# Products dealt by each step's own work, evictions in two steps, and reordered products in the prologue and MLP of a stick-breaking attention layer

## The chip, the cores and the metric

One core of a Trainium2 chip runs the whole program. The metric is the device time of one execution in microseconds (us), the median of three runs. TensorE (PE) multiplies, VectorE (DVE), ScalarE (ACT) and GpSimd (POOL) work elementwise, SyncE (SP) issues the transfers (DMAs). Matrix products are written to eight banks of PSUM of 128 x 512 floats.

## What is computed

The layer works on 2048 tokens of 1024 numbers. A combined projection gives queries, keys and values of 12 heads of 64, and queries of four heads that attend to 256 memory tokens. Its output is projected, normalised, and goes through an MLP with a squared ReLU and a second normalisation.

```python
proj = x @ w_in_sb                                   # q, k, v, q_mem
z = q_blk @ k.T * scale                              # per head, causal
log_stay = where(strict, log_sigmoid(-z), 0)
later = reverse_cumsum(log_stay) - log_stay
w = where(strict, exp(log_sigmoid(z) + later), 0)    # stick-breaking weights
mix = w @ v
mem_out = softmax(q_mem @ k_mem.T * scale) @ v_mem
x = layer_norm(ALPHA * x + concat(mix, mem_out) @ w_out)
h = square(relu(x @ w_up))
out = layer_norm(ALPHA * x + h @ w_down)
```

## The kernel before

Every operand of a product is split into two half-precision parts, high and low, and a product takes three passes (`PASSES`, line 183): high by high, high by low, low by high. So a unit of projection, 128 output columns for a chunk of 512 tokens, is 3 x 8 = 24 matmuls of 128 x 512 (`proj_cols`, line 246). Its result in PSUM is split into two half-precision tiles by two instructions, ACT for the high part and DVE for the low part, which reads the high one (`split_ps`, line 159).

**Prologue.** Memory keys and values, the transposed x of the four chunks, and for each chunk the projections of heads pair 0 (`proj_v`, `proj_k`, `proj_q`) followed by two of the eight blocks of memory attention (`mem_attend`, line 336: query projection of a block, scores, exponentials, split, transposes by DMA, value products). The order of this part is the scheduler's; inside, each engine runs its own queue in order. Weights of pair 0 are loaded in the order v, k, q; those of the memory queries are loaded when `mem_attend` is first entered.

**Attention** (`attention`, line 492) is written out by hand in steps, and each engine keeps that order. A step is one pair of heads, 128 queries and up to 512 keys: two scores into two of four banks `z` (`score`), a sigmoid by ACT (`stay`), a running product by DVE (`scan`), and in the next step the split and transpose of the weights (`spread`; by DMA, or by PE in two of four steps of a diagonal block). Four steps make a block of 512 by 512; its value products (`gather`, 24 matmuls) come `BEHIND` = 4 steps after. Six pairs of heads have 40 steps each, 10 blocks, of which four are diagonal. In iteration n stand, in this order: what was put off to n (`later`), score and sigmoid of n + 1, scan of n, spread of n - 1, and then a share of the filling work.

The filling work is projections of the next pair and, in the last two pairs, of their own later chunks and of the output (`out_proj`). It is given as segments: a list of blocks, a share `done` of the steps by which it is to be finished, and units. A step gets products in proportion to a weight:

```python
starts[len(steps)] = units, [FILL[t.i] if t.diag else 1.0 for t, _ in mine], done
...
so_far = sum(weight[:n + 1 - begin]) if n < N else full
while spent < total * min(1.0, so_far / full):
```

A unit's eviction is put off by one step: `later(1, lambda: split_ps(hi, lo, pp, ISQ))`, ACT and DVE in the same step, in front of that step's sigmoid and scan. Values take three steps: ACT copies and DVE takes differences (`copy`, line 394), ACT and POOL split, SP transposes. Two banks `pj` hold products in attention.

**MLP** (lines 785 to 946). Up and down are done by seven products in place of eight on blocks of 2 x 2, with sums before and after. `up` (line 778) uses three banks for one pair of hidden column blocks; `down` (line 866) three banks for one row of 128 tokens; sums out of PSUM are DVE's. Eight groups of weights, two halves of the tokens; in the first half the weights are also split, on ACT and DVE, and stored; in the second they are read back. The last group of each half uses eight plain products.

## Time and profile before

| | |
|---|---|
| runs | 2463.18 us median of 3 (2460.62 to 2464.71) |
| the profiled execution | 2465.01 us, its span 2463.3 us, mean granted clock 0.967 |
| busy | PE 2265.9 us, DVE 1702.5, ACT 1182.8, POOL 1034.2 |
| prologue, with the first eight steps of pair 0 | 0 to 249.1 us |
| pairs 0 (from its ninth step) to 3 | 249.1 to 764.7 us |
| last two pairs | 764.7 to 1104.8 us |
| MLP, first and second half | some 1180 to 1850 us, 1850 us to the end |

In a window's row stand its stretch and length, the busy time of PE, PE's weight loads, DVE, ACT and POOL with counts, PE's granted clock, DMA's busy share and GB/s. In a timeline's row stand start and length, engine, line, operation, tiles, count, and in brackets the idle time before it and what ended that. Lines are those of the kernel before.

### The profile page before, as it was taken

What the parts mean: (1) busy time and instruction counts of PE and PEld (TensorE: products, weight loads), DVE (VectorE), ACT (ScalarE), POOL (GpSimd) and SP (SyncE); (2) the same over time, 40 slices, a digit from 0 to 9 for tenths busy, and PEclk for the clock granted to TensorE, in tenths of its full rate; (3) what the DMA queues carried; (4) which work ended last, traced back from release to release, by engine and by line L of the source; (5) the groups of instructions that cost most, each with busy time, mean ns of one, the idle gap of its engine ahead of it and who ended that gap; (6) DMA issues with size and microseconds to landing.
All of it is one profiled execution on the core that took longest, in us unless ns stands there. A gap on an engine that the chain in (4) does not pass through costs nothing.

```text
span 2463.3 us, 34394 instructions
## 1 busy us (share of the span) xinstructions
PE 2265.9 (92%) x12032; PEld 1006.3 (41%) x12032; DVE 1702.5 (69%) x2385; ACT 1182.8 (48%) x2577; POOL 1034.2 (42%) x826
## 2 busy tenths in 40 slices
PE   7987999999989899998699999989999999999996
PEld 5433333333434344334244444434444444444442
DVE  4545777777776776887988888787676444555448
ACT  4455767676675656553544543454334222233321
POOL 0000656555564544664664565355335222211123
PEclk9998999999999999999899999999999999999998
DMA  8234888878887787877743454244466333323311
GB/s 261 41 75 88 147 159 143 160 135 150 154 152 144 157 173 161 164 162 158 249 150 119 161 175 140 95 163 167 141 172 230 103 107 99 102 87 95 107 38 69
DMA packets 606284, 342.02 MB, mean 139 GB/s; under 512 B 487840, under 2 KB 544672, under 8 KB 606112
## 3 DMA queue, kind: packets, MB, share of 16 engines
q1 hardware_dynamic: 606112, 339.84, 55.1%
q8 instruction: 94, 1.54, 0.3%
q14 instruction: 78, 0.64, 0.1%
HBM read 143.65 MB, written 77.59 MB: 90 GB/s over the span
## 4 chain that ended last, share of the span: by engine, by line
PE 45%; DVE 13%; DMA 3%; issue 3%; ACT 2%; POOL 2%; SPq 0%; DVEq 0%; POOLq 0%; ACTq 0%
PE upb L799 8%; PE dnb L875 8%; PE dnc L875 6%; PE dna L875 5%; PE upc L799 4%; PE upa L799 4%; PE op L639 4%; DVE wr L683 2%; PE dn L875 2%; DVE rt L683 2%; DVE acc L603 1%; DVE e L455 1%; PE z L272 1%; PE av L332 1%; DMA wd<-in_w_down_dram 1%
## 5 line engine op out<-in xcount | busy, mean ns | idle before, releaser
L310 POOL TENSOR_TENSOR t<-e,t 128x512 f16<-128x512 f32 (+1 forms) x384 | 431.6, 1148 | 437.5 <-ACT t L309 369.6
L890 POOL TENSOR_TENSOR acc<-acc,v 128x512 f32<-128x512 f32 x168 | 223.2, 1339 | 527.9 <-DVE acc L888 388.4
L799 PEld LDWEIGHTS <-rt 128*128 128x128 f16 x2688 | 268.3, 100 | 390.6 <-issue 86.3
L875 PEld LDWEIGHTS <-hl 128*128 128x128 f16 x2736 | 267.7, 98 | 330.3 <-DVE hl L810 5.5
L455 DVE TENSOR_TENSOR_SCAN e<-z,carry,zero 128x512 f32<-128x512 f32 x288 | 347.8, 1261 | 9.5 <-ACT z L447 8.8
L447 ACT ACTIVATE z<-z 128x512 f32<-128x512 f32 (+1 forms) x480 | 226.3, 514 | 257.6 <-PE z L272 135.9
L799 PE MATMUL upb<-op,rt 128*128 128x512 f16 x1152 | 281.6, 395 | 37.3 <-DVE u L842 28.4
L875 PE MATMUL dnb<-wr,hl 128*128 128x512 f16 x1008 | 243.8, 379 | 0.0
L272 PE MATMUL z<-k,q 64*128 64x512 f16 (+3 forms) x1440 | 195.5, 353 | 50.2 <-DVE e L455 45.5
L309 ACT ACTIVATE t<-e 128x512 f16<-128x512 f32 (+1 forms) x384 | 226.4, 616 | 13.2 <-DMA w<-t 12.2
L799 PE MATMUL upa<-op,rt 128*128 128x512 f16 x768 | 185.4, 388 | 14.9 <-ACT u L832 10.7
L799 PE MATMUL upc<-op,rt 128*128 128x512 f16 x768 | 178.8, 380 | 0.9 <-DVE u L843 0.9
L639 PE MATMUL op<-wo,mx 128*128 128x512 f16 x720 | 172.2, 388 | 1.2 <-DVE acc L646 1.2
L875 PE MATMUL dnc<-wr,hl 128*128 128x512 f16 x672 | 167.9, 379 | 1.2 <-DVE acc L886 1.0
L875 PE MATMUL dna<-wr,hl 128*128 128x512 f16 x672 | 163.8, 380 | 3.3 <-DVE hl L810 3.2
L455 DVE TENSOR_TENSOR_SCAN e<-z,zero 128x128 f32<-128x128 f32 (+1 forms) x192 | 147.0, 805 | 22.7 <-ACT z L447 16.5
L332 PE MATMUL av<-w,v 128*64 128x512 f16 (+3 forms) x1440 | 148.9, 352 | 7.1 <-DMA w<-t 5.9
L252 PE MATMUL pq<-xT,wq 128*128 128x512 f16 x576 | 142.4, 389 | 8.2 <-DVE k L162 5.0
L252 PE MATMUL vp<-xT,wv 128*128 128x512 f16 x576 | 145.6, 395 | 2.3 <-ACT wv L143 2.3
L805 ACT ACTIVATE u<-u 128x512 f32<-128x512 f32 x96 | 60.4, 629 | 164.9 <-DVE u L843 73.1
L252 PE MATMUL kp<-xT,wk 128*128 128x512 f16 x576 | 138.9, 383 | 0.0
L908 ACT ACTIVATE v<-dna 128x512 f32<-128x512 f32 x56 | 32.4, 592 | 214.9 <-POOL acc L890 210.3
(176 smaller groups left out, 3211.1 us busy)
## 6 DMA issues: line engine op xcount, KB each, us to landing
keptdown<-wr SPq DMA_DIRECT2D x106, 256.0 KB, 3.3
wr<-keptdown SPq DMA_DIRECT2D x106, 256.0 KB, 2.9
keptup<-rt SPq DMA_DIRECT2D x48, 512.0 KB, 3.1
rt<-keptup SPq DMA_DIRECT2D x48, 512.0 KB, 3.4
wu<-in_w_up_dram SPq DMA_DIRECT2D x32, 512.0 KB, 4.5
wd<-in_w_down_dram SPq DMA_DIRECT2D x32, 512.0 KB, 4.0
x<-in_x_dram SPq DMA_DIRECT2D x16, 512.0 KB, 10.3
acc<-in_x_dram SPq DMA_DIRECT2D x16, 512.0 KB, 5.4
```

The costliest lines, as they stand in the source:

```text
L252: T.matmul(pp, lhsT=wt[:, a, k, :], rhs=xs(xT, c, b, k), start=n == 0, stop=n == 3 * KT - 1)
L272: T.matmul(banks[h], lhsT=q[rows, a, i * P:(i + 1) * P], rhs=keys(b)[rows], start=n == 0, stop=stop and n == 2)
L309: A.activation(hi, src, AF.Copy)
L310: G.tensor_tensor(lo, src, hi, ALU.subtract)
L332: T.matmul(av[h * HD:(h + 1) * HD, i0 * P:].rearrange("p (t n) -> p t n", n=P), lhsT=vv(h, a), rhs=pT(h, b)[:, i0:, :], start=first and n ...
L447: A.activation(t.z[:, :t.W], t.z[:, :t.W], AF.Sigmoid, scale=-SCORE)
L455: V.tensor_tensor_scan(t.e[:, t.W - 1::-1], t.z[:, t.W - 1::-1], zero[:, 0:1].broadcast_to([P, t.W]), init, ALU.mult, ALU.add)
L639: T.matmul(pp, lhsT=lhs, rhs=W[f"o{k}"][:, kb, n * C:(n + 1) * C], start=m == 0, stop=m == 3 * NKO - 1)
L683: V.scalar_tensor_tensor(lo, src, scale, hi, ALU.mult, ALU.subtract)
L799: T.matmul(bv, lhsT=r[:, a, k, :], rhs=operand(ops, s, b, k), start=start and n == 0, stop=n == 3 * HB - 1, skip_group_check=not start)
L875: mm = T.matmul(bank, lhsT=hl[s][:, g, a, i * P:(i + 1) * P], rhs=wr[r][:, g, b, :], start=start and m == 0, stop=m == 3 * n - 1, skip_gro ...
L890: G.tensor_tensor(sl, sl, u, ALU.add)
```

## The change

Six places change. Evictions of keys and queries go through `evict`: ACT in the step after the product, DVE a step later; the difference of values moves a step later too (`diff`). Products are dealt by `deal`: each step has a time of its own (`OWN`, plus `VALUES` in the step that holds gathers) and a share, and gets what is left of a common level. Among the segments, the second chunk's keys and queries of the last two pairs move into pair 3's segment, and the last two pairs get four joined segments in place of eight. In the prologue two blocks of memory attention come ahead of a chunk's own projections, and the bank `pt` is used for products too. In `up` the third sum is made as bc + u1 and then bb, and S4 comes ahead of A22. In `down` the products of two rows alternate.

```diff
+    def evict(hi, lo, pp):
+        def high():
+            A.activation(hi, pp, AF.Copy, scale=ISQ)
+            later(1, lambda: V.scalar_tensor_tensor(lo, pp, ISQ, hi, ALU.mult, ALU.subtract))
+        later(1, high)
...
-        later(1, lambda: split_ps(hi, lo, pp, ISQ))
+        evict(hi, lo, pp)
...
+            later(1, diff)
+
+        def diff():
             V.tensor_tensor(df[:, 1:], d[:, :C - 1], d[:, 1:], ALU.subtract)
             later(1, split)
...
-    FILL = (0.45, 0.45, 0.85, 1.1)
+    SHARE = (0.62, 0.89, 0.78, 0.96), 1.0
+    OWN = (3100, 4300, 2200, 2500), 1800
+    VALUES = 4200, 6500
...
+        share = [SHARE[0][t.i] if t.diag else SHARE[1] for t, _ in steps]
+        own = [OWN[0][t.i] if t.diag else OWN[1] for t, _ in steps]
+        for n, (t, _) in enumerate(steps):
+            if t.i == TB - 1 and n + 1 + BEHIND < N:
+                own[n + 1 + BEHIND] += VALUES[0] if t.diag else VALUES[1]
+
+        def deal(begin, count, total):
+            mine = range(begin, begin + count)
+            low, high = 0, 10 * (total + sum(own))
+            for _ in range(60):
+                rate = (low + high) / 2
+                parts = [max(0, rate * share[n] - own[n]) for n in mine]
+                low, high = (rate, high) if sum(parts) < total else (low, rate)
+            return [sum(parts[:k + 1]) for k in range(count)]
...
-                while spent < total * min(1.0, so_far / full):
+                while spent < min(total, plan[min(n - begin, len(plan) - 1)]):
...
         prod(bc, S1, rt1, True)
+        u3 = sbt("et", [P, C], F32, f"u3_{nm}")
+        V.tensor_tensor(u3, bc, u1, ALU.add)
...
         prod(bb, S3, rt3, False)
-        V.tensor_tensor(u3, bb, u1, ALU.add)
-        V.tensor_tensor(u3, bc, u3, ALU.add)
+        V.tensor_tensor(u3, bb, u3, ALU.add)
+        prod(bc, S4, r22, False)
+        V.tensor_tensor(u2, bc, u2, ALU.add)
         prod(bb, A22, rt4, False)
         V.tensor_tensor(u1, bb, u1, ALU.add)
-        prod(bc, S4, r22, False)
-        V.tensor_tensor(u2, bc, u2, ALU.add)
...
+    free_banks[0] = ("pj", "pj", "pt")
     for c in range(NC):
+        for _ in range(2):
+            next(members, None)
         for fn in (proj_v, proj_k, proj_q):
             run(fn(0, c))
-        for _ in range(2):
-            next(members, None)
+    free_banks[0] = ("pj",)
...
-            units += [unit(fn, q, 0) for q in (p + 1, p + 2) for fn in (proj_k, proj_q)]
+            units += [unit(fn, q, c) for c in range(2) for q in (p + 1, p + 2) for fn in (proj_k, proj_q)]
...
+    segments.append(([(a, 0), (b, 0)], 0.9, among(kq(a, 2), 0)))
+    segments.append(([(a, 1), (b, 1)], 0.95, among(kq(b, 2), 4) + kq(a, 3)[:1] + [flat[0][0]] + kq(a, 3)[1:] + take(2)))
+    segments.append(([(a, 2), (b, 2)], 0.95, kq(b, 3) + [once(gamma)] + take(8)))
+    final = take(14)
+    segments.append(([(a, 3), (b, 3)], 0.95, final))
```

In `down` the loop over two rows i now runs once for each kind of product, in the order A11, A12, S2, S1, S3, S4, A22, where it ran A11 and A12 of each row and then the five others of each row; S1 is added to the rows of x from its bank by DVE, and u3 by POOL as before.

Counted in the order of PE, a full block of pair 1 (third chunk, last block) has 8, 9, 8 and 9 products in its four steps before; now it has 12, 3, 12 and 11, the 3 right behind the gathers. Pair 3 has 288 products before and 384 now, the last two pairs' first eight steps 91 and 43.

The first place is DVE's queue in pair 1, where the query unit of pair 2's first chunk is evicted (`q2_0` from its bank `pq2_0`) among the scans of pair 1's third chunk (`e1_2_0_i_h`: step i, head h). Before:

```order
L455 SCALAR_TENSOR_TENSOR e1_2_0_0_0_4589<-z1_2_0_0_0_4522,carry_4461,zero_76 128x512
L455 SCALAR_TENSOR_TENSOR e1_2_0_0_1_4591<-z1_2_0_0_1_4523,carry_4461,zero_76 128x512
L162 SCALAR_TENSOR_TENSOR q2_0_4478<-pq2_0_4477,q2_0_4478 128x512
L455 SCALAR_TENSOR_TENSOR e1_2_0_1_0_4625<-z1_2_0_1_0_4579,carry_4461,zero_76 128x512
L455 SCALAR_TENSOR_TENSOR e1_2_0_1_1_4627<-z1_2_0_1_1_4580,carry_4461,zero_76 128x512
```

Now:

```order
L466 SCALAR_TENSOR_TENSOR e1_2_0_0_0_4585<-z1_2_0_0_0_4513,carry_4444,zero_76 128x512
L466 SCALAR_TENSOR_TENSOR e1_2_0_0_1_4587<-z1_2_0_0_1_4514,carry_4444,zero_76 128x512
L466 SCALAR_TENSOR_TENSOR e1_2_0_1_0_4612<-z1_2_0_1_0_4575,carry_4444,zero_76 128x512
L466 SCALAR_TENSOR_TENSOR e1_2_0_1_1_4614<-z1_2_0_1_1_4576,carry_4444,zero_76 128x512
L466 SCALAR_TENSOR_TENSOR e1_2_0_2_0_4651<-z1_2_0_2_0_4602,carry_4444,zero_76 128x512
L466 SCALAR_TENSOR_TENSOR e1_2_0_2_1_4653<-z1_2_0_2_1_4603,carry_4444,zero_76 128x512
L260 SCALAR_TENSOR_TENSOR q2_0_4503<-pq2_0_4502,q2_0_4503 128x512
L466 SCALAR_TENSOR_TENSOR e1_2_0_3_0_4687<-z1_2_0_3_0_4641,carry_4444,zero_76 128x512
```

The eviction stood between the scans of steps 0 and 1 and stands between those of steps 2 and 3, since the unit ends a step later and is evicted two steps after its end.

The second place is PE's queue at the end of the prologue: the scores of the last block of memory attention (`zm1_3_3`), and the first score of attention (`z0_0_0_0_0`). Before:

```order
L272 LDWEIGHTS qm1_2_1828
L272 MATMUL zm1_3_3_2004<-kvm_83,qm1_2_1828 128x256
L272 LDWEIGHTS q0_0_648
L272 MATMUL z0_0_0_0_0_2133<-k0_0_618,q0_0_648 128x128
L272 LDWEIGHTS q0_0_648
L272 MATMUL z0_0_0_0_1_2134<-k0_0_618,q0_0_648 128x128
```

Now (the lines left out are 8 key and 24 query products of pair 0's last chunk, each with its weight load):

```order
L280 LDWEIGHTS qm1_2_1739
L280 MATMUL zm1_3_3_1915<-kvm_83,qm1_2_1739 128x256
L252 LDWEIGHTS wk0_572
L252 MATMUL kp0_3_2064<-xT03_0_506,wk0_572 128x512
...
L252 LDWEIGHTS wq0_577
L252 MATMUL pq0_3_2091<-xT03_1_536,wq0_577 128x512
L280 LDWEIGHTS q0_0_944
L280 MATMUL z0_0_0_0_0_2133<-k0_0_914,q0_0_944 128x128
```

Nothing stood between the last memory scores and attention; now 32 products do.

The third place is DVE's queue in the MLP's first half, third group: splits of down weights (`wr`) and up weights (`rt`), and the additions of the third sum (`u3`) from the banks `upb` and `upc`. Before:

```order
L683 SCALAR_TENSOR_TENSOR wr0_4_4_14259<-t2_d0_5_14634,wr0_4_4_14259 128x512
L683 SCALAR_TENSOR_TENSOR wr0_4_6_14261<-t4_d0_4_14435,wr0_4_6_14261 128x512
L683 SCALAR_TENSOR_TENSOR wr0_4_5_14260<-t3_d0_5_14636,wr0_4_5_14260 128x512
L683 SCALAR_TENSOR_TENSOR wr0_4_6_14261<-t4_d0_5_14638,wr0_4_6_14261 128x512
L683 SCALAR_TENSOR_TENSOR rt0_6_14926<-wu0_6_0_14914,rt0_6_14926 128x512
L810 TENSOR_TENSOR hl0_4_0_14248<-r_0_4_14355,hl0_4_0_14248 128x512
L842 TENSOR_TENSOR u3_0_4_14372<-upb0_4_14301,u1_0_4_14315 128x512
L843 TENSOR_TENSOR u3_0_4_14372<-upc0_4_14302,u3_0_4_14372 128x512
```

Now:

```order
L714 SCALAR_TENSOR_TENSOR wr0_4_4_14259<-t2_d0_5_14634,wr0_4_4_14259 128x512
L714 SCALAR_TENSOR_TENSOR wr0_4_6_14261<-t4_d0_4_14435,wr0_4_6_14261 128x512
L869 TENSOR_TENSOR u3_0_4_14343<-upc0_4_14302,u1_0_4_14315 128x512
L714 SCALAR_TENSOR_TENSOR wr0_4_5_14260<-t3_d0_5_14636,wr0_4_5_14260 128x512
L714 SCALAR_TENSOR_TENSOR wr0_4_6_14261<-t4_d0_5_14638,wr0_4_6_14261 128x512
L714 SCALAR_TENSOR_TENSOR rt0_6_14926<-wu0_6_0_14914,rt0_6_14926 128x512
L841 TENSOR_TENSOR hl0_4_0_14248<-r_0_4_14357,hl0_4_0_14248 128x512
L874 TENSOR_TENSOR u3_0_4_14343<-upb0_4_14301,u3_0_4_14343 128x512
```

The addition from `upc` moved ahead of three splits; the one from `upb` stands behind the same splits as before.

## Rows read from the trace of the kernel before

**Rows 1.** The page, part 1: busy us, share of the span, instructions.

```profile
PE 2265.9 (92%) x12032; PEld 1006.3 (41%) x12032; DVE 1702.5 (69%) x2385; ACT 1182.8 (48%) x2577; POOL 1034.2 (42%) x826
```

**Rows 2.** Windows of the prologue; columns as told above.

```profile
90.00:191.00 101.00, 89.24 (x484) 39.73 (x481) 55.59 (x158) 54.66 (x164) 3.56 (x3) 0.92 0.41 78
191.00:249.10 58.10, 40.07 (x243) 17.75 (x243) 32.47 (x79) 32.25 (x98) 7.49 (x7) 0.79 0.40 82
```

**Rows 3.** Windows of pairs 0, 1, 2 and 3.

```profile
249.10:356.10 107.00, 100.32 (x652) 40.50 (x649) 82.95 (x88) 77.06 (x192) 66.85 (x60) 1.00 0.87 159
356.10:490.40 134.30, 124.29 (x824) 51.36 (x822) 100.76 (x117) 93.23 (x239) 79.77 (x73) 1.00 0.83 150
490.40:624.40 134.00, 125.56 (x834) 51.95 (x831) 99.49 (x116) 92.37 (x238) 79.76 (x73) 1.00 0.80 146
624.40:764.70 140.30, 127.87 (x811) 51.54 (x812) 104.92 (x117) 97.12 (x252) 84.83 (x77) 0.96 0.83 153
```

**Rows 4.** Windows of the last two pairs: steps 1-8, 9-24, 25-48, 49-80.

```profile
764.70:799.40 34.70, 32.97 (x219) 14.94 (x216) 20.80 (x33) 16.91 (x40) 11.16 (x11) 1.00 0.60 131
799.40:858.80 59.40, 50.09 (x339) 22.11 (x336) 45.11 (x53) 38.43 (x92) 30.88 (x28) 0.94 0.70 153
858.80:956.50 97.70, 97.53 (x604) 41.61 (x604) 67.63 (x81) 52.88 (x136) 45.57 (x42) 1.00 0.87 173
956.50:1104.80 148.30, 138.21 (x784) 56.45 (x784) 119.36 (x153) 82.81 (x192) 89.05 (x74) 0.97 0.75 155
```

**Rows 5.** Windows of the MLP's first and second half.

```profile
1300.00:1850.00 550.00, 518.48 (x2355) 234.62 (x2354) 442.68 (x587) 244.05 (x426) 252.64 (x173) 0.97 0.45 147
...
1920.00:2390.00 470.00, 470.00 (x2180) 213.05 (x2178) 229.03 (x355) 132.07 (x227) 99.95 (x80) 1.00 0.30 96
```

**Rows 6.** Waits of the whole span: us in total, times, longest us.

```profile
DVE q L162 <- ACT q L161: 71.1, 23, 7.7
...
PE z L272 <- DVE e L455: 45.5, 62, 3.1
...
PE pt L319 <- DVE w L162: 15.0, 15, 4.2
```

**Rows 7.** Timeline of pair 1, 423 to 430 us, ACT, DVE and PE.

```profile
423.39 1.07 ACT L447 ACTIVATE z<-z 128x512 f32<-128x512 f32 x2 [2.19 <-PE z L272]
...
425.58 0.60 ACT L161 ACTIVATE q<-pq 128x512 f16<-128x512 f32 x1
...
426.21 0.69 DVE L162 SCALAR_TENSOR_TENSOR q<-pq,q 128x512 f16<-128x512 f32 x1 [3.37 <-ACT q L161]
...
429.32 0.82 PE L272 MATMUL z<-k,q 64*128 64x512 f16 x5 [0.79 <-DVE e L455]
```

**Rows 8.** Timeline of pair 1, 405 to 411 us, PE.

```profile
405.38 2.78 PE L332 MATMUL av<-w,v 128*64 128x512 f16 x24
408.09 0.82 PE L272 MATMUL z<-k,q 64*128 64x512 f16 x6
408.84 2.12 PE L252 MATMUL kp<-xT,wk 128*128 128x512 f16 x9
410.89 0.82 PE L272 MATMUL z<-k,q 64*128 64x512 f16 x6
```

**Rows 9.** Timelines of the prologue, PE and ACT.

```profile
38.98 5.31 PE L252 MATMUL vp<-xT,wv 128*128 128x512 f16 x16 [2.29 <-ACT wv L143]
...
45.40 1.06 ACT L143 ACTIVATE wqm<-sqm 128x1024 f16<-128x1024 f32 x1 [2.77 <-DMA sqm<-in_w_in_sb_dram]
...
82.28 0.72 PE L272 MATMUL zm<-kvm,qm 64*128 64x256 f16 x7
...
108.98 1.48 PE L332 MATMUL avm<-pm,kvm 128*64 128x512 f16 x11
...
234.15 1.48 PE L332 MATMUL avm<-pm,kvm 128*64 128x512 f16 x11
```

**Rows 10.** Timeline of the MLP's first half, third group, PE.

```profile
1380.53 4.44 PE L799 MATMUL upb<-op,rt 128*128 128x512 f16 x12 [4.53 <-DVE u L842]
```

More of the change, by code (lines that the diff above doesn't have):

```diff
@@ L500, in attention @@
                     for i in range(TB)]
-            starts[len(steps)] = units, [FILL[t.i] if t.diag else 1.0 for t, _ in mine], done
+            starts[len(steps)] = units, len(mine), done
             steps += mine
         N = len(steps)
+        share = [SHARE[0][t.i] if t.diag else SHARE[1] for t, _ in steps]
[11 more added lines that the diff above has]
+            return [sum(parts[:k + 1]) for k in range(count)]
         work, spent, total = None, 0, 0
@@ L509, in attention @@
                     run(work)
-                units, weight, done = starts[n]
-                begin, spent, total, full = n, 0, sum(k for k, _ in units), sum(weight) * done
+                units, count, done = starts[n]
+                begin, spent, total = n, 0, sum(k for k, _ in units)
+                plan = deal(n, count, total / done)
                 work = (cost for _, u in units for cost in u())
@@ L526, in attention @@
             if work is not None:
-                so_far = sum(weight[:n + 1 - begin]) if n < N else full
-                while spent < total * min(1.0, so_far / full):
+                while spent < min(total, plan[min(n - begin, len(plan) - 1)]):
                     cost = next(work, None)
@@ new lines, in down @@
+            for i in two:
+                bc[i] = pst("bk", f"dnc{half}_{i}")
+                prod(i, bc[i], S1, T1, True)
+                add(i, c1, 1, bc[i], None)
+            for i in two:
+                prod(i, bb[i], S3, T3, False)
+                u3[i] = sbt("et", [P, C], F32, f"v3_{half}_{i}")
+                V.tensor_tensor(u3[i], bb[i], u1[i], ALU.add)
+                sl = acc[c1 * TB + i][:, C:]
+                G.tensor_tensor(sl, sl, u3[i], ALU.add)
+            for i in two:
+                prod(i, bc[i], S4, B22, False)
+                add(i, c0, 1, bc[i], u2[i])
@@ L927, in down @@
+            for i in two:
+                prod(i, bb[i], A22, T4, False)
+                add(i, c1, 0, bb[i], u1[i])
             yield
```

51 lines of the change are left out of this document (16 added, 35 removed).

## The prediction

> **What bounds the kernel now.** I read the page first, then the windows stage by stage, then the waits and timelines inside the stages. On the whole TensorE (PE) is busy 92% of the span and VectorE (DVE) 69% [rows 1], so time can come from PE's idle 197 us, from clock lost behind idle, and from nothing else unless the work itself shrinks, which it does not here. The windows say where that lies. In the prologue, from 90 to 249.1 us, PE is idle 11.8 and 18.0 us, at granted clocks of 0.92 and 0.79, means of the two levels 2.4 and 1.2 GHz [rows 2]. In pairs 0 to 3 (249.1 to 764.7 us) it is idle 6.7, 10.0, 8.4 and 12.4 us [rows 3]. In the last two pairs it is idle 1.7, 9.3, 0.2 and 10.1 us [rows 4]. In the MLP's first half 31.5 of 550 us are idle, in its second half none [rows 5]. The reader is to see that attention is nearly bound by PE, but that its idle comes in a regular way, and that 858.8 to 956.5 us shows the same loop with no idle at all.
>
> What makes the idle in attention is told by the waits: PE's scores wait 45.5 us for DVE's scans (a score bank comes free when its scan ends), and DVE waits 71.1 us in q's evictions alone for ScalarE (ACT) [rows 6]. One such place in full [rows 7]: the sigmoid of a score ends at 424.46 us (423.39 + 1.07), but DVE's queue holds an eviction in front of the scan, whose ACT half starts only at 425.58; so DVE idles 3.37 us, the scan starts at 426.8 instead of 424.5, and the score at 429.32 us finds its bank late.
>
> **The change, part by part.** I make the sum against the profiled execution, 2465.0 us (its span is 2463.3), which is 1.8 us above the median of the runs, 2463.2.
>
> *Evictions in two steps, and difference of values a step later* (`evict`, `diff`). Nothing is added: the same ACT and DVE instructions, DVE's half one step later. Queued behind the waiting DVE half was the scan, and behind that the score's bank. After the change the ACT half has a whole step (3.35 us, 134.3 over 40 [rows 3]) to get done. The price is that the product's bank is held one step longer; that is the fourth rival.
>
> *Products dealt by own work* (`deal`). The counts in the order of PE are my evidence: in full blocks of pair 1 the products per step were 8 to 10 in all four steps, also in the step whose gathers take PE another 2.71 us; now that step gets none to 3 and the others 7 to 12. PE's work per block stays: four scores at 0.75, gathers at 2.71, and products at 2.05 / 9 = 0.228 us each [rows 8]; for the block's some 34 products that is 3.0 + 2.7 + 7.8 = 13.5 us, while DVE has 100.8 / 134.3 of that time to fill [rows 3]. So the two parts together can take PE's idle, not more. In pairs 0 to 2 that idle is 25.1 us. Diagonal blocks keep some: PE's transposes wait for DVE there 15.0 us in 15 waits over the program [rows 6], and these are not touched. I leave 10 us: **-15**. Bounds: 0 (the waits only change place) and -25.
>
> *Second chunks moved into pair 3's segment, the last two pairs' segments joined.* Four units of 24 products move, 96. Pair 3: 127.9 us of PE, less 5.1 for its clock of 0.96 coming back, plus 96 x 0.228 = 21.9, plus 4.6 of idle left, is 149.3 against 140.3: **+9**. Last two pairs: PE's 33.0 + 50.1 + 97.5 + 138.2 = 318.8 us [rows 4], less 101 products (five more are left to the tail) at 0.228 = 23.0, less 3 of the some 7 us that the clocks of 0.94 and 0.97 cost, plus 11 of idle left of 21.3, is 303.8 against 340.1: **-36**. The five products in the tail: **+1**. Bounds for the three together: idle all left, clock as now, -1; idle all gone and clock full, -46. I take a value nearer the second, because the stretch at 858.8 shows the loop with 0.2 us of idle under a like load. The weight loads that move with the units go through SP and ACT at four per eight steps; DMA is busy 0.60 in the stretch that gets them and 0.87 where PE has no idle [rows 4], so I cost them at nothing; without that cover one cast on ACT is 1.06 us [rows 9], 8.5 us for eight.
>
> *Memory attention ahead of each chunk's own products, and a third bank for products.* Two effects. The first product now reads the memory queries' weights, which are loaded last: their cast runs at 45.40 to 46.46 us, while the first product runs at 38.98 now [rows 9]. The 24 products of that time come later, 24 x 0.2156 (470 us over 2180 in the MLP's second half [rows 5]) = +5.2. The other effect is the chain of the eight memory blocks (exponentials, split, transposes by DMA, values): their value products run from 108.98 to 234.15 us, seven intervals of 17.9 us [rows 9], and the kernel can't leave the prologue before the last. In the changed order the first block's scores stand behind 96 products from 46.5 us, so at 46.5 + 20.7 + some 5 of transposes = 72 us. Now they begin at 82.28 us [rows 9], and the chain starts some 10 us earlier (the 5.2 is in that). Between neighbouring blocks stand 61 to 63 products, 13.4 us, and a block's values, 1.48, with its scores taken as long: 16.4 us where 17.9 is now, seven times, is another 10. Against that the first attention steps still share ACT with the last two blocks. I take **-18** for the prologue. Bounds: +5 (the late weights alone) and -45 (idle of 29.8 us, and 89.2 x 0.08 + 40.1 x 0.21 = 15.5 us of clock [rows 2]).
>
> *MLP, up.* The third sum is now made as two additions at other places; the same count. In the first half PE stalls once per group of weights, 4.53 us in the row [rows 10], for an addition that stands behind four and more splits in DVE's queue (the third place in the order). In the changed order that addition stands behind the same splits, and an earlier one, for the product now in front, behind some of them; PE has 25 products between the two ends as before. So the stall is split in two and not removed: **0**, between +5 (one more DVE instruction, as long as the 0.69 of [rows 7], in front, seven times) and -10 (the shorter stalls on the second addition). *MLP, down.* The products of two rows alternate; PE hardly waits in these now, and in the second half not at all: **0**, hidden by a PE that is busy 470 of 470 us; if it were not, one exposed addition of 0.69 us per pair of rows, 28 times, would be +19.
>
> Sum: -15 + 9 - 36 + 1 - 18 = **-59**: 2406 for an execution like the profiled one, **2404** for the median.
>
> **The rivals.** (1) *Busy is not the floor.* Products in a row are 0.2156 us apart in the MLP [rows 5] and 0.228 in attention [rows 8], because every change of kind leaves a small hole that counts as busy. If steps with no products save that for the 2,000 or so products in attention, another 25 us go: 2379. The Trainium skill says in Perfetto Trace Analysis, Identifying the Most-Contended Engine, that busy time of matmuls is no good measure of the distance to the roof because they are pipelined; by that rule this case is the likelier, but our row at 858.8 with 97.5 us for 604 matmuls shows the holes staying where PE never idles. Chance 0.12.
>
> (2) *The chain of memory blocks stays as it is.* Each block's ACT work waits in ACT's queue for the block before; if the interval stays at 17.9 and the late weights eat the earlier start, the prologue gives 0: 2422. For it: the interval is as long at 191 to 235 us, where PE has little to do. Against: there, attention's first steps share ACT. Chance 0.13.
>
> (3) *The waits change place in attention.* With no products after the gathers, PE holds no score for 12 x 0.228 + 2.71 + 0.75 = 6.2 us; then DVE must catch up, and an eviction of 0.69 us before the scan is felt. Half of attention's 41 us would be left: 2424. Chance 0.10.
>
> (4) *Slower.* A product's bank is now held a step longer, and there are two. A unit of 24 products takes 2 steps at 12 per step, and its eviction two more, so a bank turns round in four steps, just as often as it is asked for; at 15 per step, as in pair 3, it is asked for sooner. If each of the 40 key and query units in attention then stalls PE by 2.5 us, +100: 2504. It decides from 1.5 us per unit on, where the 59 are gone. Against: the mean is 7 to 10 products a step. The Trainium skill (the same page, Optimization Strategy) warns that bubbles repeated in a regular way can mean too few PSUM buffers, which is this rival's mechanism; the trace has such bubbles on score banks [rows 6] and none named on product banks in attention. Chance 0.05. (5) *Nothing to measure*: gains and new stalls cancel, 2463. Chance 0.05.
>
> **How the numbers follow.** The forecast has 0.55, with a range of its own of 2386 to 2420 (the bounds of the prologue and of the last pairs, half used each). A measurement tells 0.2%, 4.9 us, from no change. Faster: 0.55 + 0.12 + 0.13 + 0.10 = 0.90; same 0.05; slower 0.05. From 2376 to 2440 takes in the forecast, and rivals 1 to 3 each by itself, not 2 and 3 together (2443), and leaves out some 0.15.
>
> **What would show it.** In the changed profile: DVE's waits for ACT in q and k, 71.1 us for q now, under 30; scores waiting for scans under 25 us; idle of PE in pairs 1 and 2 under 5 us each, pairs 1 and 2 near 128 us; pair 3 longer, near 149; from its end to the last scan near 304. The first product at 46 us, not 39; the last memory block's values near 213 us, not 234. In the MLP's first half a stall per group as now. I am wrong if PE waits for evictions at the first product of units (rival 4), if the memory blocks still end after 228 us, or if the MLP moves by over 10 us.

## The result, and the profile after

The changed kernel takes 2437.4 us (median of six executions, 2425.1 to 2442.7); the kernel before took 2463.9 beside it. The ratio is 0.989, with a 95% interval of 0.987 to 0.991: faster by 27 us where 59 were forecast. The sign held and the time lies inside the range. The size does not hold: attention, which carried most of the sum, gave less than half of its part, and other terms missed in both directions.

The profiled execution took 2425.1 us, its span 2423.4. It is the fastest of the six, so it shows 40 us of gain where the median shows 27; the experiments explain most of that. First the page's part 1, beside [rows 1]:

```profile
PE 2235.5 (92%) x12032; PEld 999.4 (41%) x12032; DVE 1700.9 (70%) x2385; ACT 1186.9 (49%) x2577; POOL 1022.0 (42%) x826
```

Then the windows, with the columns of [rows 2]: two of the prologue, pairs 0 to 3, four of the last two pairs, the MLP's first half, and everything behind the last scan.

```profile
90.00:180.00 90.00, 82.17 (x471) 36.86 (x470) 51.22 (x150) 52.78 (x163) 3.46 (x3) 0.96 0.43 82
180.00:237.60 57.60, 47.13 (x296) 21.19 (x296) 38.37 (x88) 36.50 (x106) 6.72 (x7) 0.97 0.47 94
237.60:344.90 107.30, 102.31 (x674) 42.48 (x676) 85.18 (x90) 77.01 (x197) 68.83 (x63) 0.98 0.88 159
344.90:477.10 132.20, 123.88 (x832) 52.35 (x829) 101.36 (x117) 92.42 (x239) 79.53 (x72) 1.00 0.86 152
477.10:606.00 128.90, 121.25 (x819) 51.53 (x819) 100.19 (x116) 91.38 (x238) 79.52 (x73) 1.00 0.83 152
606.00:760.00 154.00, 143.31 (x906) 60.30 (x903) 109.24 (x122) 98.90 (x255) 87.07 (x77) 0.98 0.76 138
760.00:791.20 31.20, 26.42 (x189) 12.29 (x190) 18.49 (x30) 16.32 (x39) 12.03 (x12) 0.95 0.64 135
791.20:846.10 54.90, 52.10 (x349) 22.57 (x344) 47.93 (x57) 38.81 (x93) 28.27 (x26) 1.00 0.90 203
846.10:937.30 91.20, 89.53 (x577) 37.90 (x576) 67.57 (x89) 54.79 (x139) 47.76 (x44) 1.00 0.90 182
937.30:1076.70 139.40, 127.56 (x731) 50.95 (x728) 114.69 (x140) 78.38 (x187) 87.50 (x73) 0.95 0.76 149
1275.00:1825.00 550.00, 518.48 (x2400) 236.24 (x2399) 447.27 (x618) 253.28 (x434) 252.66 (x179) 0.99 0.45 150
1076.70:2423.40 1346.70, 1253.86 (x5790) 569.68 (x5790) 926.85 (x1341) 515.25 (x869) 519.80 (x375) 0.98 0.42 136
```

Against [rows 3, 4] the reader sees four things. The ninth step of pair 0, the first behind the prologue's windows, comes at 237.6 us and not at 249.1. Pairs 0 to 2 gain 0, 2 and 5 us. Pair 3 grows by 13.7 us and the last two pairs shrink by 23.4 (340.1 to 316.7). In pair 3 and the last two pairs PE is still idle 10.7 and 21.1 us: products moved, idle did not go. And in the MLP's first half the same 518.48 us of PE hold 2400 products where 2355 were [rows 5], at a granted clock of 0.99 and not 0.97.

The waits of PE in the whole span (us in total, times, longest), beside [rows 6]:

```profile
PE pt L327 <- DVE w L162: 39.5, 23, 7.7
PE upc L830 <- DVE u L869: 15.4, 6, 2.7
PE z L280 <- DVE e L466: 13.4, 19, 1.7
```

and DVE's for the first halves of the two evictions:

```profile
DVE k L260 <- ACT k L259: 5.4, 5, 1.5
DVE q L260 <- ACT q L259: 4.8, 7, 1.2
```

DVE's wait for ACT in q's eviction fell from 71.1 to 4.8 us and the scores' wait for scans from 45.5 to 13.4, both as forecast. But PE's transposes of the diagonal weights (`pt`) now wait 39.5 us where they waited 15.0. The longest of these stands in the timeline of pair 3, SP, ACT, DVE and PE:

```profile
650.91 0.39 PE L327 MATMUL pt<-idf,e 128*128 128x128 f32 x2
...
652.49 0.57 SPq L138 DMA_DIRECT2D sk<-in_w_in_sb_dram  x1
...
656.91 1.06 ACT L143 ACTIVATE wk<-sk 128x1024 f16<-128x1024 f32 x1 [4.00 <-DMA sk<-in_w_in_sb_dram]
...
660.17 0.26 ACT L161 ACTIVATE w<-pt 128x128 f16<-128x128 f32 x1
...
660.46 0.29 DVE L162 SCALAR_TENSOR_TENSOR w<-pt,w 128x128 f16<-128x128 f32 x1 [8.54 <-ACT w L161]
...
661.53 0.87 PE L327 MATMUL pt<-idf,e 128*128 128x128 f32 x3 [7.74 <-DVE w L162]
```

The transposes at 650.91 fill the one bank `pt`. It comes free when ACT and DVE have split it, but in ACT's queue two casts of the key and query weights of one of the last pairs stand in front, and the first waits 4.00 us for its DMA. So the split runs at 660.17 and the next transposes at 661.53. Two more, of 3.5 us behind casts of the output's weights and of 5.2 us behind the layer norm's work, come about in this manner; the other 19 in attention are of 0.2 to 2.2 us.

### The profile page after: what moved, and what is told of

Its sections match the earlier page's. It is cut to its first block, busy times and chain, and to the rows that moved or that the text cites. A ratio compares the mean times of both kernels' runs of the same rounds, so it can differ in the third digit from the quotient of the medians.

```text
span 2423.4 us, 34527 instructions
## 1 busy us (share of the span) xinstructions
PE 2235.5 (92%) x12032; PEld 999.4 (41%) x12032; DVE 1700.9 (70%) x2385; ACT 1186.9 (49%) x2577; POOL 1022.0 (42%) x826
## 4 chain that ended last, share of the span: by engine, by line
PE 45%; DVE 13%; issue 4%; ACT 4%; DMA 3%; POOL 2%; SPq 1%; DVEq 0%; ACTq 0%; POOLq 0%
PE upb L830 7%; PE dnb L906 7%; PE dnc L906 5%; PE dna L906 5%; PE op L670 5%; PE upc L830 5%; PE upa L830 4%; DVE wr L714 2%; PE z L280 2%; PE av L340 2%; DVE rt L714 2%; DMA wd<-in_w_down_dram 1%; PE pq L252 1%; DVE acc L634 1%; PE kp L252 1%
## 5 line engine op out<-in xcount | busy, mean ns | idle before, releaser
L921 POOL TENSOR_TENSOR acc<-acc,v 128x512 f32<-128x512 f32 x112 | 149.9, 1342 | 488.9 <-DVE acc L919 432.4
L830 PE MATMUL upb<-op,rt 128*128 128x512 f16 x1152 | 268.1, 381 | 14.8 <-DVE u L874 8.3
L906 PE MATMUL dnb<-wr,hl 128*128 128x512 f16 x1008 | 235.9, 379 | 0.0
L280 PE MATMUL z<-k,q 64*128 64x512 f16 (+3 forms) x1440 | 184.3, 349 | 14.4 <-DVE e L466 13.4
L906 PE MATMUL dnc<-wr,hl 128*128 128x512 f16 x672 | 161.1, 379 | 1.0 <-DVE acc L917 0.7
L906 PE MATMUL dna<-wr,hl 128*128 128x512 f16 x672 | 154.4, 379 | 0.0
L252 PE MATMUL vp<-xT,wv 128*128 128x512 f16 x576 | 138.2, 384 | 0.0
L418 POOL TENSOR_TENSOR vt<-ve,vt 128x512 f16<-128x512 f32 x24 | 28.4, 1185 | 209.2 <-ACT vt L417 202.7
## 6 DMA issues: line engine op xcount, KB each, us to landing
x<-in_x_dram SPq DMA_DIRECT2D x16, 512.0 KB, 10.4
```

The lines of the kernel that those rows point to most:

```text
L252: T.matmul(pp, lhsT=wt[:, a, k, :], rhs=xs(xT, c, b, k), start=n == 0, stop=n == 3 * KT - 1)
L280: T.matmul(banks[h], lhsT=q[rows, a, i * P:(i + 1) * P], rhs=keys(b)[rows], start=n == 0, stop=stop and n == 2)
L830: T.matmul(bv, lhsT=r[:, a, k, :], rhs=operand(ops, s, b, k), start=start and n == 0, stop=n == 3 * HB - 1, skip_group_check=not start)
L906: mm = T.matmul(bank, lhsT=hl[s][:, g, a, i * P:(i + 1) * P], rhs=wr[r][:, g, b, :], start=start and m == 0, stop=m == 3 * n - 1, skip_gro ...
L921: G.tensor_tensor(sl, sl, u, ALU.add)
```

## The experiments

Each was timed beside the kernel before, which measured 2461.0 to 2463.1 us (2459.3 by one execution in the last set). "Behind the last scan" is the time from the last scan of attention to the end, in the profile.

**Is the first profile typical?** No edit, a second profile.

> The changed kernel again, nothing altered: the reference for the other runs on this chip. Theory A (the profiled execution of the changed kernel, 2425.1, was a lucky one and the typical one is its median, 2437.4): about 2437, and a second profile whose stages differ from the first by up to 12 us, spread over many places. Theory B (the first profile is typical and the median was pulled up by the chip): 2425 or so.

Measured: 2434.4 (2418.2 to 2442.6; ratio 0.9859 to 0.9906), and again the profiled execution was the fastest. Its attention agrees within 2 us with the first profile's, so no spread over many places, and neither theory as it was put: what differs between executions lies elsewhere. Two more executions, at the end, show where the larger part of it lies (below).

**Transposes behind the products.**

```diff
+            held = 0 <= n - 1 < N and steps[n - 1][0].diag and steps[n - 1][0].i not in DMA_DIAG
             if 0 <= n - 1 < N:
-                spread(steps[n - 1])
+                if not held:
+                    spread(steps[n - 1])
...
                 if n >= N:
                     run(work)
+            if held:
+                spread(steps[n - 1])
```

> The changed kernel, with one edit: in the first two steps of a diagonal block TensorE's transposes of the stick-breaking weights are issued after the step's products instead of before them. Theory A (the gain in attention was given back at these transposes, which waited 39.5 us for the split that frees their bank, where they waited 15.0 before the change): that wait falls under 20 us and the kernel gains 10 to 20 us on the changed kernel. Theory B (VectorE and ScalarE are late there anyhow, and a transpose that waits only shows it first): the wait goes to the next scores or to the gathers, and the time stays within 4 us. Theory C (the transposes' result is needed soon, four steps later): the gathers wait and it gets slower by 5 or more.

Measured: 2422.8 (ratio 0.9814 to 0.9858), 12 us below the changed kernel. In attention the transposes' wait fell from 35.0 to 13.0 us, the scores' rose from 10.4 to 19.4, and attention from the ninth step on took 829.3 us in place of 839.1. Theory A. In pairs 0 to 2 alone the transposes' wait fell from 11.3 us, in ten waits, to 1.0 us in two.

**The split first in its step.**

```diff
-        later(1, split)
+        due.setdefault(clock[0] + 1, []).insert(0, split)
```

> The changed kernel, with one edit: the split of the transposed weights, which frees their bank, is put first among the work that falls due in its step, so that casts of weights and the layer norm stand behind it in ScalarE's and VectorE's queues. Theory A (three or four long waits of 3.5 to 7.7 us come from a cast that stands in front of the split and waits for a weight's DMA): the longest wait of the transposes falls under 3 us, their sum by about 15 us, the time by 10 to 15. Theory B (the blocked queue itself is what costs; sigmoids stand behind the same cast): the wait moves to the scores, the time stays within 4 us.

Measured: 2427.3 (0.9848 to 0.9873); the transposes' longest wait is 1.1 us, their sum 13.5, but the scores wait 24.2, so attention gains only 5.5 us (833.6). Between A and B: of the 21.5 us that the transposes wait less, the scores wait 13.8 more. In pairs 0 to 2 the transposes' ten waits stay, at 9.1 us, so the work due ahead of the split in its step is not what makes these; with the transposes behind the products they go, as the run before shows.

**The MLP as before the change**: `up` and `down` put back whole, of which this is the third sum.

```diff
-        V.tensor_tensor(u3, bc, u1, ALU.add)
...
-        V.tensor_tensor(u3, bb, u3, ALU.add)
+        V.tensor_tensor(u3, bb, u1, ALU.add)
+        V.tensor_tensor(u3, bc, u3, ALU.add)
```

> The changed kernel with the MLP's two functions (sums in the up product, order of rows in the down product) as they were before the change. My forecast said that these are worth 0 (+5 to -10). The two profiles show the stretch behind the last scan 11.8 us shorter after the change. Theory A (that is the reordered additions): undoing them costs 8 to 14 us. Theory B (it is the run, its clock, or the shorter tail of attention): undoing them changes nothing beyond 4 us.

Measured: 2438.1 (0.9890 to 0.9916), 3.7 us above the changed kernel: by that number theory B. But its executions lie within 2.2 us of each other, where the changed kernel's lie 24 apart, and it needs 1358.2 us behind the last scan, as the kernel before (1358.5).

**Prologue, evictions, dealing, segments, undone one by one.**

```diff
-    free_banks[0] = ("pj", "pj", "pt")
     for c in range(NC):
-        for _ in range(2):
-            next(members, None)
         for fn in (proj_v, proj_k, proj_q):
             run(fn(0, c))
+        for _ in range(2):
+            next(members, None)
-    free_banks[0] = ("pj",)
```

> The changed kernel, with the prologue as before: each chunk's own products ahead of the memory blocks, and one kind of bank for products. Theory A (the prologue's part is a gain of its own, 11.5 us by the two profiles, where I forecast 18): 8 to 14 us slower than the changed kernel, first attention step at 249 us and not at 237. Theory B (it is given back later, since the first attention steps share ScalarE with the last memory blocks): within 4 us.

```diff
     def evict(hi, lo, pp):
-        def high():
...
-        later(1, high)
+        later(1, lambda: split_ps(hi, lo, pp, ISQ))
```

(keys and queries both go through `evict`; and the difference of values in the step of its copy)

> The changed kernel, with the evictions of keys and queries and the difference of values in one step again. Theory A (the eviction's two halves in one step are what made VectorE wait for ScalarE and so the scores for the scans): scores wait over 35 us for scans again (13 in the changed kernel) and it is 8 to 20 us slower than the changed kernel. Theory B (the dealing alone took those waits away): scores stay under 25 us and the time within 4 us. Theory C (with the dealing, the one-step eviction relieves the transposes): up to 8 us faster.

```diff
+    FILL = (0.45, 0.45, 0.85, 1.1)
...
-                while spent < min(total, plan[min(n - begin, len(plan) - 1)]):
+                so_far = sum(weight[:n + 1 - begin]) if n < N else full
+                while spent < total * min(1.0, so_far / full):
```

> The changed kernel, with the products dealt out by the old weights of a step (0.45, 0.45, 0.85, 1.1 in a diagonal block, 1.0 elsewhere); evictions and segments as changed. Theory A (the dealing gives the steps that gather no products and so removes waits for the scans): scores wait over 25 us, pairs 1 and 2 take 133 us or more each, 6 to 15 us slower than the changed kernel. Theory B (the dealing mostly moves the wait from the scores to the diagonal transposes): the transposes wait 15 to 20 us in place of 39.5, the scores 30 or more, time within 5 us.

```diff
-            units += [unit(fn, q, c) for c in range(2) for q in (p + 1, p + 2) for fn in (proj_k, proj_q)]
+            units += [unit(fn, q, 0) for q in (p + 1, p + 2) for fn in (proj_k, proj_q)]
...
-    segments.append(([(a, 0), (b, 0)], 0.9, among(kq(a, 2), 0)))
...
+    segments.append(([(a, 0)], 0.7, among(kq(a, 1), 0)))
+    segments.append(([(b, 0)], 0.7, among(kq(b, 1), 2)))
...
```

> The changed kernel, with the old segments: one chunk of one of the last two pairs in each, and the second chunks not moved to pair 3. Theory A (joining and moving is worth what the last 120 steps show, 13.6 us more in pair 3 and 23 less in the last two pairs): 6 to 14 us slower than the changed kernel, pair 3 near 140 us. Theory B (with evictions and dealing in place the last pairs have little idle to give): within 4 us.

Measured: prologue 2434.6, evictions 2456.8, dealing 2427.6, segments 2423.0, against 2434.4. Only the evictions are plain: 22 us slower without them, attention 861.1 us, scores waiting 34.9 us, theory A but for the size. With the old dealing the transposes wait 23.0 us and the scores 13.1, with the old segments 18.9 and 24.7. Undoing either seemed to make the kernel faster, by 7 and 11 us, which fits neither of their theories, and undoing the prologue to change nothing (theory B by the number), but executions of all four scattered; those without the two-step evictions fell into two groups, 2442 to 2446 and 2456 to 2460.

**What scatters them.** Three of the profiles so far showed one subtraction of 13.8 us on VectorE. The changed kernel itself shows it in the two last executions. Of the second, DVE, POOL and PE between the MLP's halves, and line 841's row of durations (min, median, max in ns):

```profile
1836.68 1.29 POOL L634 TENSOR_TENSOR acc<-acc,gb 128x512 f32<-128x512 f32 x1
...
1836.90 13.81 DVE L841 TENSOR_TENSOR hl<-r,hl 128x512 f16<-128x512 f32 x1 [8.70 <-ACT r L839]
...
1837.90 2.51 POOL L628 TENSOR_TENSOR acc<-acc,gb 128x512 f32<-128x512 f32 x2
...
1840.35 9.81 POOL L634 TENSOR_TENSOR acc<-acc,gb 128x512 f32<-128x512 f32 x8
...
1850.77 1.03 PE L906 MATMUL dna<-wr,hl 128*128 128x512 f16 x2 [9.23 <-DVE hl L841]
```

```profile
L841 DVE TENSOR_TENSOR hl<-r,hl x32: 678/692/13812, 1184.2 to 2372.5; 128x512 f16<-128x512 f32 x32
```

and the same place in the first profile of the changed kernel:

```profile
1832.39 0.86 DVE L841 TENSOR_TENSOR hl<-r,hl 128x512 f16<-128x512 f32 x1 [9.44 <-ACT r L839]
1832.67 2.95 POOL L628 TENSOR_TENSOR acc<-acc,gb 128x512 f32<-128x512 f32 x2
```

> The changed kernel, unaltered, a third profile. The first two (2425.1 and 2418.2) are below its median and show no hold. Theory A (the hold is what the slower executions have): if this execution takes over 2430, a VectorE subtraction of 13.8 us between the MLP's halves and 1352 us or more behind the last scan; if it takes less, none and 1347 or less. Theory B (something else makes them slow): over 2430 without the hold.

> The changed kernel, unaltered, a fourth profile. As for the third: theory A, over 2430 with the hold and under 2430 without it; theory B, over 2430 without it.

Measured: 2435.5 and 2439.7, both with the hold, and 1356.5 and 1356.7 us behind the last scan. Theory A. Of the ten profiles with the changed MLP and these normalized rows, five have the hold and 1352.3 to 1359.3 us behind the last scan, five have none and 1342.8 to 1346.7. In the five without, the subtraction also began while a GpSimd instruction ran, and ended 0.55 us after that one: 0.86 us long in two, 1.61 us in three, of which the kernel with the old prologue is one:

```profile
1841.44 1.27 POOL L634 TENSOR_TENSOR acc<-acc,gb 128x512 f32<-128x512 f32 x1
1841.66 1.61 DVE L841 TENSOR_TENSOR hl<-r,hl 128x512 f16<-128x512 f32 x1 [8.69 <-ACT r L839]
```

The hold is not all of the scatter: in the last execution attention took 845.7 us, 6.6 more than in the first profile, and why is not shown.

**Taking the hold away.** Four of the eight rows that are normalized there have gain and shift on VectorE:

```diff
-            if tb < NT // 2 or tb % TB < TB - 1:
+            if (tb < NT // 2 and not tb % 2) or (tb >= NT // 2 and tb % TB < TB - 1):
```

> The changed kernel, with one edit: of the eight rows that are normalized between the MLP's halves, four have their gain and shift on VectorE (two instructions a half row) and not on GpSimd. In three profiles one VectorE subtraction took 13.8 us where it takes 0.69, from the time that GpSimd worked without a break until GpSimd's queue was empty, and TensorE waited 9.3 us for it; in the other six it did not. Theory A (this hold is what makes executions of one and the same kernel differ by some 13 us): no such subtraction, executions within 6 us of each other, median 2420 to 2428. Theory B (the spread is the clock's, elsewhere): spread as in the changed kernel (24 us over 12 runs), median within 4 us of 2434. Theory C (16 more VectorE instructions in a stretch where it is on the path): slower by 3 to 8.

Measured: 2422.2 (2417.7 to 2424.3, 6.6 us apart; ratio 0.9822 to 0.9855), no hold. Theory A. In all six kernels with this edit and the changed MLP the profile shows none. That fits with GpSimd's long run as what the hold needs.

**The evictions alone, on the kernel before**: `evict` and `diff` of the change, nothing else.

> The kernel before, with one part of the change alone: evictions of keys and queries in two steps, and the difference of values a step later. Undone in the changed kernel, this part cost some 22 us. Theory A (this part is nearly the whole gain): 15 to 25 us faster than the kernel before, DVE's waits for ScalarE in keys and queries gone, scores' wait for scans from 45.5 to under 25. Theory B (it pays only with the dealing, which gives the halves a step of their own): under 8 us.

Measured: 2442.8, ratio 0.991 to 0.9937, so 18.2 us of gain by this part alone: theory A, but the scores still wait 26.6 us, over the 25 named, and DVE 21.2 for ACT in q. Attention takes 834.3 us from the ninth step on, less than in the changed kernel:

```profile
249.10:1104.80 855.70, 796.85 (x5047) 330.45 (x5045) 641.02 (x748) 550.81 (x1379) 487.88 (x431) 0.98 0.80 154
```

is the kernel before, and the evictions alone are

```profile
246.30:1080.60 834.30, 790.18 (x5071) 331.12 (x5067) 645.58 (x749) 550.66 (x1382) 493.97 (x433) 0.99 0.82 158
```

**The parts once more, without the hold.** Each of the next three is the kernel of 2422.2 us with a part undone, by the edits shown above: dealing and segments together, prologue, MLP.

> The changed kernel with four of the eight rows normalized on VectorE (measured at 2422.2, without the hold), and dealing and segments both as before: what is left of the change is the two-step evictions, the prologue and the MLP. My forecast gave dealing and segments, with the evictions, -42 in attention. Theory A (they bring nothing beside the evictions: attention was 834.3 us in the kernel before with the evictions alone, 839.1 in the changed one): 2413 to 2424, attention near 834. Theory B (they bring what the last pairs' shorter stretch shows, 13 us): 2430 or more.

> The changed kernel with four rows normalized on VectorE, and the prologue as before. Without the hold's scatter this should tell what the first undoing could not (2434.6 against 2434.4). Theory A (the prologue's part is worth the 6.6 us by which the first attention step came later there): 2427 to 2433. Theory B (given back in attention): 2420 to 2425.

> The changed kernel with four rows normalized on VectorE, and the MLP's two functions as before. Theory A (the reordered sums are worth the difference of the stretches behind the last scan, 1358.2 with the old functions and 1341 to 1347 with the new where no hold fell): 2433 to 2440. Theory B (the rows on VectorE take the same stall away, whatever the sums' order): 2420 to 2426.

Measured: 2416.1 (ratio 0.9785 to 0.9822), 2431.3 (0.9855 to 0.9891) and 2433.3 (0.9867 to 0.9896); theory A each time, though the first's attention is 840.2 us and not 834. The prologue brings 9 us, the MLP 11. Dealing and segments bring nothing: 6 us by the medians against them, 0.6 by the spans of the profiles. Their attention in the profile, with the changed order and with the old one:

```profile
236.00:1074.50 838.50, 783.79 (x5056) 329.74 (x5050) 642.88 (x749) 547.94 (x1381) 488.83 (x433) 0.98 0.82 156
```

```profile
238.70:1078.90 840.20, 795.32 (x5071) 332.42 (x5067) 645.16 (x749) 549.89 (x1382) 494.12 (x433) 0.98 0.81 157
```

With the changed order PE is busy 11.5 us less, for 15 matmuls fewer in the record, some 3 us at 0.228 each (why the rest is not shown), and idle 9.8 us more; behind the last scan it needs 1341.4 against 1336.4 us. The waits of PE in attention, changed order and then old:

```profile
PE pt L327 <- DVE w L162: 35.5, 21, 7.7
PE z L280 <- DVE e L466: 11.9, 17, 1.0
```

```profile
PE z L280 <- DVE e L466: 23.8, 32, 2.3
PE pt L327 <- DVE w L162: 10.0, 15, 2.5
```

Where which part does this is told by stretches. The waits of PE in pairs 0 to 2, with the evictions alone and in the changed kernel:

```profile
PE z L280 <- DVE e L466: 4.7, 8, 1.0
PE pt L327 <- DVE w L162: 4.1, 10, 0.8
```

```profile
PE pt L327 <- DVE w L162: 11.3, 10, 1.4
PE z L280 <- DVE e L466: 5.2, 7, 0.9
```

The kernel before has 17.9 us of the scores and 4.8 of the transposes there, and the changed kernel with the old dealing 4.9 and 4.1. So in these pairs the evictions took the scores' waits and the dealing brought the transposes'. In pair 3 and the last two pairs the scores wait 24.5 us before, 19.7 with the evictions alone, 19.0 with all but the segments and 5.3 with all; the transposes 5.6, 4.9, 7.8 and 22.7. There the segments did most of both.

**Versions that beat both.** Both edits to the transposes and the four rows on VectorE, together; then the same with the old segments, and with old segments and old dealing.

> The changed kernel with three edits together: transposes after the products in a diagonal block's first two steps, their split first in its step, and four of the eight rows between the MLP's halves normalized on VectorE. By the parts (attention 8 to 10 us shorter with the first, 4 to 5 with the second, up to 10 by the third): Theory A (they add up): 2408 to 2415. Theory B (the first two relieve the same wait, and one of them is enough): 2415 to 2422. Theory C (nothing left to gain, TensorE is the bound): 2422 or more.

> The same three edits, on the changed kernel with the old segments (one chunk of one of the last two pairs in each, second chunks not moved to pair 3). The old segments measured 2423 where the changed kernel measured 2434, though their attention was only 2 us shorter in the profile. Theory A (the new segments cost something real, and it is not the hold): 5 to 11 us faster than the run with three edits. Theory B (the 11 us were the share of executions with the hold): within 4 us of it.

> The three edits (transposes late, their split first, four rows on VectorE) with dealing and segments both as before. Theory A (dealing and segments bring nothing, and the transposes' two edits are worth 10 us on any order): 2405 to 2413, at or below the 2411.7 of the three edits alone. Theory B (the two edits only mend what the dealing brought to the diagonal blocks): 2413 to 2422, no better than without them.

Measured: 2411.7 (2408.5 to 2412.0; ratio 0.9779 to 0.9808), 2410.7 (0.9776 to 0.9814) and 2416.2 (0.9794 to 0.9825). The parts add up (theory A for the first, attention 828.1 us). The new segments bring nothing here either (theory B for the second). The edits to the transposes mend what dealing and segments brought and give nothing on the old order, where 2416.1 had been measured without them (theory B for the third). The first is 23 us below the changed kernel's 2434.4, and 4.5 below the third, whose interval overlaps its own.

## Why the prediction was right and wrong

The failed part is attention. Its three terms, -15, +9 and -36, make -42; from the ninth step on it went from 855.7 to 839.1 us, -16.6, and the evictions alone took it to 834.3, -21.4. What I expected beyond that, from dealing and joined segments, did not come.

**Evictions: right in mechanism.** The scan no longer stands behind a half-done eviction. They alone brought 18 us, two thirds of all that was measured, for which the sum had no term of their own. The bank held a step longer (rival 4) cost 0.2 us.

**"I leave 10 us" of idle in pairs 0 to 2: wrong.** The step that failed is the sentence that the transposes' waits "are not touched". Idle there is 21.0 us (107.30 + 132.20 + 128.90 less PE's 347.44), and 11.3 of it, in ten waits, stand before the transposes. The evictions alone had left 17.5 us of idle (370.1 us with 352.62 of PE) and 4.1 of these waits; the dealing brought 7 us of waits to the transposes and took none from the scores. That is rival 3, waits that change place, but at a bank that I had named and called untouched, and not after the gathers.

**Pair 3 +9, last two pairs -36: the moved products were right, the idle was not.** The last two pairs lost 23.4 us, which is the 23.0 of moved products and nothing more: idle stayed at 21.1 us where I let 21.3 fall to 11. Pair 3 has 143.3 us of PE (I had 144.7 without idle) and 10.7 idle where I left 4.6. (The bound of -1 left the tail out: 21.9 - 23.0 + 1.1 is 0.) I took one stretch without idle as the pattern for all, and no row showed that the others could follow it. I also costed the moved weight loads at nothing; the 3.5 us wait stands behind casts of theirs. The 7.7 us wait stands behind a cast that pair 3 had before, too; with the old segments no transposes wait over 1.4 us in that pair.

**Prologue -18: half.** The first product of the memory queries came at 46.7 us, as forecast at 46. The blocks follow each other at 16.7 us, where I had 16.4:

```profile
46.73 5.49 PE L252 MATMUL pqm<-xT,wqm 128*128 128x512 f16 x16 [1.17 <-ACT wqm L143]
...
84.78 1.77 PE L280 MATMUL zm<-kvm,qm 64*128 64x256 f16 x24 [0.69 <-ACT qm L259]
...
107.46 1.48 PE L340 MATMUL avm<-pm,kvm 128*64 128x512 f16 x11
...
224.55 1.46 PE L340 MATMUL avm<-pm,kvm 128*64 128x512 f16 x11 [0.86 <-DMA pm<-w]
```

The step that failed is the start: I put the first block's scores at 72 us, they came at 84.78 (82.28 before), so those 10 us were not there. I had costed the 96 products at the full clock and let the transposes of x go through in 5 us. From the first product to these scores the window shows a granted clock of 0.82, and 6.4 us of idle, of which 5.6 are four waits for DVE's splits of the transposed x:

```profile
46.70:84.80 38.10, 31.73 (x142) 15.79 (x144) 12.12 (x18) 9.82 (x17) 0.00 (x0) 0.82 0.13 37
```

The intervals' 8 us are most of what the undoing measures as 9.

**MLP 0: wrong, by 11 us.** The split of the stall was foreseen, its price was not. Timeline of the first half after, PE, to be held against [rows 10]:

```profile
1423.23 2.75 PE L830 MATMUL upc<-op,rt 128*128 128x512 f16 x12 [2.52 <-DVE u L869]
1429.92 5.12 PE L830 MATMUL upb<-op,rt 128*128 128x512 f16 x23 [1.57 <-DVE u L874]
```

The two stalls, 4.1 us together, are hardly shorter than the 4.53 of [rows 10]. But there twelve products after the stall took 4.44 us, and here they take 2.75, as in four of the five groups. The window on those products in the kernel before shows why:

```profile
1380.50:1385.00 4.50, 4.47 (x13) 1.70 (x13) 3.08 (x5) 3.45 (x7) 0.50 (x1) 0.62 0.58 224
```

The granted clock is 0.62 there, a mean of its two levels, 1.2 and 2.4 GHz; behind the first of the shorter stalls it is 1.00:

```profile
1423.20:1426.00 2.80, 2.77 (x13) 1.27 (x13) 2.80 (x3) 0.00 (x0) 2.72 (x3) 1.00 1.02 363
```

I had the row with 4.44 us before me and read only the 4.53 in its bracket. The two runs without the hold, MLP as before and as changed, give the sizes in the first half:

```profile
1278.40:1828.40 550.00, 516.80 (x2360) 234.54 (x2359) 445.81 (x596) 242.21 (x426) 246.81 (x168) 0.97 0.45 150
1274.50:1824.50 550.00, 522.78 (x2422) 238.36 (x2421) 456.75 (x630) 249.70 (x431) 244.08 (x172) 0.99 0.46 152
```

The 62 products more are worth 13.4 us at 0.2156 each: 7.4 come from the pace (beyond 0.2156 for each product PE was busy 8.0 us and now 0.6) and 6.0 from idle (33.2 us and now 27.2). `up` and `down` were undone only together, but PE waits 0.7 and 0.2 us for DVE before `down`'s products there, so nearly all of this is `up`'s.

**Not foreseen: the hold.** In five of ten profiles it costs some 11 us behind the last scan. It is most of why the median shows 27 us where the fastest execution shows 40, and with it the MLP's 11 us were all but gone in the median.

As a sum: evictions -18, prologue -9, MLP -11, dealing and segments 0 to +6, the hold +11 in about half of the profiles. That is -21 to -38, with -27 measured. That the time lies in the stated range is partly luck: -42 in attention was 25 too much and -18 for the prologue 9, and the MLP's 11 us, which the sum had at 0, made up for some of it.

**What would show it, point by point:** waits for q under 30 (4.8) and scores under 25 (13.4) came true, as did the first product. Pairs 1 and 2 with under 5 us of idle (8.3 and 7.6), pair 3 at 149 (154.0), the last pairs at 304 (316.7) and the last memory values at 213 (224.55) did not; and the MLP moved by over 10 us, which I had named as proof against me.

## What to carry to other kernels

Dealing work out anew can move waits from one bank to the next that is freed by the same two queues: list every bank whose release stands in ScalarE's and VectorE's queue, and what is in front of it there, a cast that waits for a DMA above all. Read a stall together with the speed of the products behind it: two shorter stalls of nearly the same sum were a gain here by themselves. And when executions of one kernel scatter, look for a single instruction with a maximum far over its median, before trusting differences smaller than the scatter.

## What the runs showed of the hardware

A VectorE subtraction with both inputs in SBUF took 13.81 us in place of 0.69: it began 0.2 us into a GpSimd instruction of 1.29 us and ended 0.55 us after the last of GpSimd's run of ten more. In two executions of the same kernel it took 0.86 us and ended 0.55 us after the one GpSimd instruction that ran when it began; so it did in three kernels with a part undone, with 1.61 us. The Trainium skill, SBUF — State Buffer, says in the section Who interferes with whom that a VectorE instruction with two SBUF inputs contends with a GpSimd instruction that reads SBUF, and in the section SBUF: two separate sides that whichever starts first has the shared pair of ports for the whole instruction while the other is fully blocked. The five short ones agree with that. In the five long ones the block lasted for a whole unbroken run of GpSimd instructions, and of that these sections say nothing. Three of the short ones began 0.2 us into a GpSimd instruction like the long ones, so that does not decide it, and what does stays open.

TensorE stood still for 4.2 to 5.7 us before a twelve of `up` products once per group, in the kernel before and in the two changed ones with the old MLP, and the twelve took 4.3 to 5.3 us. Of the ten stalls of 2.5 to 2.75 us there, in the changed kernel's first profile and in the kernel with four rows on VectorE, seven were followed by twelve products in 2.75 us and three by twelve in 4.2 to 4.4. The length of the stall alone does not say which.
